# A two-layer attention and GLA trunk: small products of the first three head pairs at five stated places, rows of the position terms fetched between the first pass's loads

## The chip, the cores and the metric

The kernel runs on one core of one Trainium2 chip. The metric is the device time of one execution in microseconds (us); the kernel before takes 761.03 us, the median of 3 runs (760.69 to 761.86).

The engines are called by their names in the profile: PE is TensorE (matrix products, PEld its weight loads), DVE VectorE, ACT ScalarE, POOL GpSimd, SP SyncE, which here issues nearly all DMAs.

## The reference, cut to what matters

A trunk of two layers over 256 tokens with 1,024 features. Each layer is a token mixer and a gated FFN with a short convolution; both are modulated by terms computed from a vector c (a 1,024 x 12,288 product over both layers, of which each column is one dot product per output). Layer 0 mixes tokens by attention: 16 heads of width 64 in 3 groups, where group 0 sees every earlier token up to 128 back, and groups 1 and 2 see every 4th and every 16th. The change touches this attention.

```python
qkv = (h @ w_in).reshape(B, S, A_GROUPS, 3, A_HEADS, A_HEAD_DIM)
...
s = jnp.einsum('bnqrhe,bnkrhe->bnrhqk', qb, kk).astype(jnp.float32) + bias[None, None, None]
s = jnp.where(mask[None, :, None, None], s, NEG_INF)
m = jnp.max(s, axis=-1, keepdims=True)
p = jnp.exp(s - m)
den = jnp.sum(p, axis=-1)
o = jnp.einsum('bnrhqk,bnkrhe->bnqrhe', p, vv.astype(jnp.float32))
...
wts = jax.nn.softmax(jnp.stack(lses), axis=0)
o = jnp.sum(wts[..., None] * jnp.stack(outs), axis=0)
return o.reshape(B, S, A_WIDTH).astype(h.dtype) @ w_out
```

The bias is a table lookup by distance (the position terms). Layer 1 mixes by gated linear attention, which the change leaves alone. The FFN is `u = h @ w_up`, a 3-tap convolution along the tokens, `(silu(a) * b) @ w_down`.

## The kernel before

**Products.** Each large fp32 product is made of three products of parts: a factor is split into a high part (rounded, by a cast on ACT, `whi`, L176) and the rest (`wlo`, a subtraction on DVE, L182 or in two halves by `low_part`, L188), and `mm3` (L203 to L205) adds high by high, high by low and low by high. So every weight that is loaded costs one cast on ACT and one subtraction on DVE before the second and third product. Weights arrive through four buffers `raw` by SP's queue.

**Pairs.** The 16 heads are worked as 8 pairs u (the loop `for u in range(NPAIR)`, L665). For a pair the large products give q and k of each of the three groups g (PSUM tiles `pqk`, over 8 blocks kt of 128 features) and v (`pv`, two banks of 128 tokens). The small products follow: `scores` (L484) gives the four score tiles `s` (two heads by two halves of the tokens; shared and rest for group 0, L496 and L501, 64 x 64 pieces of groups 1 and 2, L511), adds the position terms and takes maxima on DVE (L531), exponentiates on ACT (L550) and normalises on DVE (`pn`, L542, L543); `turn` (L565) or `turn_all` (L579) transposes pn on PE into PSUM banks `t`, which ACT and DVE copy to `pt` (L567, L583); `outputs` multiplies pt by v (`po`, L592, L596) and splits the result (L603, L604).

**First pass** (L670 to L703). Pair 0 whole and q, k of pair 1 are computed together over kt, while the inputs h are made block by block. For each kt SP loads 1,024 KB of the modulation's weights (`ada_raw`, L135) and 960 KB of `w0` (L169). DVE makes two dot products with c (L142), the scaled block xr (L287), the low part of the first half of w0 (L188), the low part of h (L291), and the low part of the second half. ACT makes the two terms `mod` (L150 from the first dot, L152 from the second), the casts of the two halves, and hhi (L289).

**After it.** u=1 has only v left (48 products over 384 columns). u=2 has three groups of q and k (48 products over 256 columns each) and v; from u=3 on each pair has the same, with its small products in fixed places: `turn_all` of the pair before after group 1, and `scores` of the pair and `outputs` of the pair before, after v. For the first three pairs the small products stand at some ten places between those of other pairs. DVE also works off the remaining dot products, three after groups 0 and 2 (`next_half`).

**What sets the order.** A scheduler places the instructions on each engine, from their dependencies and the order of the program's text; `behind(...)` (L276) and `tc.issue_after` state that an instruction is not placed ahead of another on the queue. So the order in the text moves things that the text does not name.

**Position terms.** `rows` holds for each head one line of 768 terms; it goes to device memory (`rows_d`, L442) and is read back by `load_bias` (L370) so that each partition gets its own shift: for each half-head two DMAs of 64.5 KB (L379) and two of 32 KB (L380). Before, the store and the 16 DMAs of pairs 0 and 1 follow all loads of the first pass and the two of v's weights.

**FFN** (`ffn`). The first tile of w_up lies at columns 112 and 640 of a shared buffer; copies of h for kt 6 and 7 (`level`) are used in two of 22 blocks.

## Time and profile before

| | |
|---|---|
| median of 3 runs | 761.03 us (760.69 to 761.86) |
| the profiled execution | 761.25 us |
| its span, from the first to the last instruction | 759.5 us |
| PE busy | 750.5 us, 99% |
| DVE, ACT, POOL busy | 649.7, 484.9, 31.9 us |
| read from HBM | 185.06 MB, 245 GB/s over the span |
| granted TensorE clock | 0.999 |
| first pass | 13.6 to 56.7 us of the span |
| from there to the first product of u=3 | 56.7 to 104.2 us |

The times in the profile count from the start of the span. A timeline row gives start, length, engine, line, operation, what is written and read, and in brackets the idle time ahead of it and what ended that. A group's row gives the count, the busy time and the mean of one in ns, and the idle time ahead of the group with its releasers. Neighbouring rows of one engine overlap by some 0.1 us, since an instruction starts before the one ahead is fully out.

### The profile page before, as it was taken

The numbers are of one execution on the slowest core, as the hardware profiler recorded it, in microseconds if no ns is written. First come the engines' busy times: TensorE is split into PE (matmuls) and PEld (weight loads), VectorE is DVE, ScalarE is ACT, GpSimd is POOL, SyncE is SP. The second block draws the span as 40 slices with busy tenths as digits, with TensorE's granted clock in tenths as the row PEclk, the third lists the DMA queues.
The fourth block names the chain that finished last, engine by engine and source line by source line (L and its number), as shares of the span: only waits on it lengthen the run. The fifth ranks groups of instructions, "written<-read, shape, count | busy, mean of one in ns | idle before, by whom it ended". The sixth has DMA issues, their size and how long they took to land.

```text
span 759.5 us, 16068 instructions
## 1 busy us (share of the span) xinstructions
PE 750.5 (99%) x6416; PEld 732.3 (96%) x6416; DVE 649.7 (86%) x1190; ACT 484.9 (64%) x951; POOL 31.9 (4%) x57
## 2 busy tenths in 40 slices
PE   8999999999999999999999999999999999999997
PEld 6999899999999999999999999999999999999996
DVE  6997999888989679999999868987868999998592
ACT  6466666565556478676767556836867866676551
POOL 0001101101101010000000000000010000000100
PEclk9999999999999999999999999999999999999999
DMA  8988888878887357877646986864646777774621
GB/s 349 405 287 304 325 300 324 277 263 309 275 286 257 112 189 274 318 268 242 230 143 235 365 278 219 337 227 176 213 168 229 248 261 269 208 174 156 205 99 56
DMA packets 39481, 187.20 MB, mean 246 GB/s; under 512 B 9020, under 2 KB 11708, under 8 KB 25838
## 3 DMA queue, kind: packets, MB, share of 16 engines
q1 hardware_dynamic: 39024, 185.73, 70.4%
q8 instruction: 50, 0.82, 0.4%
q10 hardware_dynamic: 382, 0.45, 0.2%
q14 instruction: 25, 0.20, 0.1%
HBM read 185.06 MB, written 1.10 MB: 245 GB/s over the span
## 4 chain that ended last, share of the span: by engine, by line
PE 83%; DMA 7%; DVE 6%; ACT 2%; issue 1%; SPq 0%; ACTq 0%; DVEq 0%
PE pab L204 10%; PE pab L205 10%; PE pab L203 10%; PE pqk L203 5%; PE pqk L205 5%; PE pqk L204 4%; PE pd L204 4%; PE pd L205 4%; PE pd L203 4%; PE pv L203 3%; PE pv L205 3%; PE pv L204 3%; DMA raw<-in_w 2%; PE py L203 2%; PE py L205 2%; PE py L204 2%
## 5 line engine op out<-in xcount | busy, mean ns | idle before, releaser
L176 ACT CAST whi<-raw 128x1024 fp32r<-128x1024 f32 (+4 forms) x262 | 236.9, 948 | 100.8 <-PE pab L204 44.6
L182 DVE TENSOR_TENSOR wlo<-raw,whi 128x1024 fp32r<-128x1024 f32 (+5 forms) x246 | 263.2, 1096 | 37.3 <-ACT whi L176 36.5
L204 PE MATMUL pab<-hlo,whi 128*128 128x256 f32 x672 | 185.0, 277 | 0.0
L205 PE MATMUL pab<-hhi,wlo 128*128 128x256 f32 x672 | 184.9, 277 | 0.0
L203 PE MATMUL pab<-hhi,whi 128*128 128x256 f32 x672 | 183.5, 277 | 0.0
L204 PEld LDWEIGHTS pab<-hlo,whi 128*128 128x128 f32 x672 | 126.2, 188 | 0.2
L205 PEld LDWEIGHTS pab<-hhi,wlo 128*128 128x128 f32 x672 | 126.2, 188 | 0.0
L203 PEld LDWEIGHTS pab<-hhi,whi 128*128 128x128 f32 x672 | 125.2, 188 | 0.1
L142 DVE CUSTOM_DVE_ANT_0 ada_raw<-ada_raw,c_bc 128x1024 f32<-128x1024 f32 x96 | 114.3, 1233 | 3.2 <-DMA ada_raw<-in_w_ada 3.0
L203 PE MATMUL pqk<-hhi,whi 128*128 128x256 f32 x374 | 102.4, 279 | 0.0
L204 PE MATMUL pqk<-hlo,whi 128*128 128x256 f32 x374 | 102.0, 278 | 0.0
L205 PE MATMUL pqk<-hhi,wlo 128*128 128x256 f32 x374 | 101.6, 279 | 0.2 <-DVE wlo L182 0.2
L205 PE MATMUL pd<-ghi,wlo 128*128 128x256 f32 x308 | 84.8, 276 | 0.0
L204 PE MATMUL pd<-glo,whi 128*128 128x256 f32 x308 | 84.8, 276 | 0.0
L203 PE MATMUL pd<-ghi,whi 128*128 128x256 f32 x308 | 84.7, 276 | 0.0
L205 PEld LDWEIGHTS pqk<-hhi,wlo 128*128 128x128 f32 x374 | 69.2, 188 | 1.1 <-issue 0.7
L203 PEld LDWEIGHTS pqk<-hhi,whi 128*128 128x128 f32 x374 | 69.9, 188 | 0.2 <-ACT v L642 0.2
L204 PEld LDWEIGHTS pqk<-hlo,whi 128*128 128x128 f32 x374 | 69.9, 188 | 0.1
L205 PEld LDWEIGHTS pd<-ghi,wlo 128*128 128x128 f32 x308 | 57.7, 188 | 0.0
L204 PEld LDWEIGHTS pd<-glo,whi 128*128 128x128 f32 x308 | 57.7, 188 | 0.0
L203 PEld LDWEIGHTS pd<-ghi,whi 128*128 128x128 f32 x308 | 57.7, 188 | 0.0
L203 PE MATMUL pv<-whi,hhi 128*128 128x384 f32 (+2 forms) x160 | 53.1, 337 | 0.6 <-DVE k L616 0.3
(275 smaller groups left out, 1473.6 us busy)
## 6 DMA issues: line engine op xcount, KB each, us to landing
raw<-in_w_up SPq DMA_DIRECT2D x42, 1024.0 KB, 5.0
ada_raw<-in_w_ada SPq DMA_DIRECT2D x29, 1024.0 KB, 5.9
raw<-in_w_down SPq DMA_DIRECT2D x28, 704.0 KB, 4.4
ada_raw<-in_w_ada SPq DMA_DIRECT2D x38, 512.0 KB, 6.7
raw<-in_wqk SPq DMA_DIRECT2D x18, 1024.0 KB, 6.6
raw<-in_wv SPq DMA_DIRECT2D x14, 768.0 KB, 6.7
raw<-in_w SPq DMA_DIRECT2D x7, 960.0 KB, 6.5
raw<-in_w_v_b SPq DMA_DIRECT2D x6, 768.0 KB, 5.4
```

What stands on the lines that cost most here:

```text
L142: i = nc.vector.tensor_tensor_reduce(w, w, c_bc, op0=ALU.mult, op1=ALU.add, scale=1.0, scalar=0.0, accum_out=dot,)
L176: copied[0] = nc.scalar.copy(part(hi[:, c]), part(raw[:, c]))
L182: last_lo[0] = nc.vector.tensor_tensor(part(lo[:, c]), part(raw[:, c]), part(hi[:, c].bitcast(F32)), op=ALU.subtract)
L203: mm(ps, a[0], b[0], start=start, stop=False)
L204: mm(ps, a[0], b[1], start=False, stop=False)
L205: return mm(ps, a[1], b[0], start=False, stop=stop)
```

## The change

The store of the rows is issued after w0 of kt 2, and the four DMAs of one half-head after w0 of kt 3, 4, 5 and 6 each: pair 0's two half-heads, then pair 1's. In the loop, the small products of the first three pairs are stated at five places: scores of pair 0 after v of u=1; scores of pair 1 after group 0 of u=2; the transposes of pair 0 after group 1; those of pair 1 after group 2; and after v of u=2 the scores of pair 2 and the outputs of pairs 0 and 1. The normalisation of row 3 is no longer held back for the first two pairs. In the FFN the first tile of w_up lies at column 0, the copies of h are made for kt 6 alone, and in the two blocks that use them kt 6 is taken third.

```diff
@@ -365,13 +365,18 @@
     shift(att, 32)
     rows = att.tile([16, NROW], F32, tag="pt", name="rows")
 
-    def load_bias(u):
+    biases = [[], []]
+
+    first = []
+
+    def load_bias(u, heads=range(2)):
 
         both = []
         r = rows_d[:, :]
-        first = None if u else att.tile([P, 4, KEYS], F32, tag="pt", name="bias")
-        for hh in range(2):
-            b = (first[:, 2 * hh : 2 * hh + 2, :].rearrange("p a b -> p (a b)")[:, 0 : KEYS + 2] if u == 0
+        if u == 0 and 0 in heads:
+            first.append(att.tile([P, 4, KEYS], F32, tag="pt", name="bias"))
+        for hh in heads:
+            b = (first[0][:, 2 * hh : 2 * hh + 2, :].rearrange("p a b -> p (a b)")[:, 0 : KEYS + 2] if u == 0
                  else att.tile([P, KEYS + 2], F32, tag=f"bias{hh}", name="bias", bufs=1)[:, :])
             at = r.offset + (2 * u + hh) * NROW
             for x in range(2):
@@ -438,8 +443,13 @@
         if kt == 1:
             with behind(last):
                 last = scale_terms(1)
+        with tc.issue_after(last_load[0].ins):
+            if kt == 2:
+                nc.sync.dma_start(rows_d, rows)
+            elif 3 <= kt < 7:
+                u, hh = divmod(kt - 3, 2)
+                biases[u] += load_bias(u, (hh,))
     with tc.issue_after(last_load[0].ins):
-        nc.sync.dma_start(rows_d, rows)
         nc.sync.dma_start(small[:, C_CW:], I["small"][:, C_CW:])
 
     KO = 6
@@ -481,7 +491,7 @@
     last_pv, last_s, last_cast = [], [None], [None]
     OLEVEL = 5
 
-    def scores(u, q, k, v, bias):
+    def scores(u, q, k, v, bias, *after):
 
 
         m = tmp.tile([P, 16], F32, tag="m", name="m")
@@ -500,38 +510,36 @@
             e = slice(E * hh, E * hh + E)
             return mm(s[:, 0:n], qs[e, hh, P * (i // 2) : P * (i // 2) + P], kl[e, 0:n], start=False, stop=True)
 
-        def dilated(s, tiles):
+        def dilated(s):
...
 
 
 
-        for tiles in ((0, 1, 2), (3,)) if u == 0 else (range(4),):
-            s = {i: bank("s", "t" if i == 3 and u else "s") for i in tiles}
...
+        s = {i: bank("s", "t" if i == 3 else "s") for i in range(4)}
+        for i in range(4):
+            with behind(*after):
+                last = shared(s[i], i)
...
         pn = []
 
         def normalised():
@@ -550,7 +558,7 @@
                 exps.append(nc.scalar.activation(c, c, AF.Exp, bias=m[:, 4 + r : 5 + r], accum_out=m[:, 8 + r : 9 + r]))
             nc.vector.reciprocal(m[:, 12:16][:, rs], m[:, 8:12][:, rs])
             for r in (2 * hh, 2 * hh + 1):
-                if r < 3:
+                if u == 0 or u > 1 and r < 3:
                     normalised()
         return v, pn, normalised
 
@@ -565,7 +573,7 @@
                     last_t[0] = nc.tensor.transpose(t[:, c], pn[r][:, c], ident)
             with behind(*(evacuated if after else [])):
                 turned.append((nc.vector.tensor_copy if r % 2 else nc.scalar.copy)(pt[:, r, :], t[:, 0:KEYS]))
-            if r == 0:
+            if r == 0 and len(pn) < 4:
                 normalised()
 
     def turn_all(of, pt, *after):
@@ -577,7 +585,7 @@
             for i, (r, j) in enumerate(blocks[4 * n : 4 * n + 4]):
                 with behind(*after):
                     last_t[0] = nc.tensor.transpose(t[:, P * i : P * i + P], pn[r][:, P * j : P * j + P], ident)
-                if (r, j) == (0, 2):
+                if (r, j) == (0, 2) and len(pn) < 4:
                     normalised()
             with behind(*evacuated):
                 turned.append((nc.vector.tensor_copy if n == 1 else nc.scalar.copy)(flat[:, 512 * n : 512 * n + 512], t))
@@ -664,8 +672,7 @@
 
     for u in range(NPAIR):
         if u < 2:
-            with tc.issue_after(last_load[0].ins):
-                bias = load_bias(u)
+            bias = biases[u]
         place = u % 2 if u < 4 else 1
         if u == 0:
             k_hi, k_lo = ([att.tile([P, T + 4 * (i or j)], F32R, tag=f"k0{i}{j}", name="k", bufs=1) for j in range(2)] for i in range(2))
@@ -707,20 +714,22 @@
                     s, e = kt == 0, kt == KT - 1
 
 
-                    if u == 2 and (g, kt) == (1, 6):
-                        turn(before, pt := new_pt(), 0)
-                    at_t = u > 2 and (g, kt) == (2, 0)
                     hk = level if (u, g) > (3, 1) and g != 1 and kt == 0 else h[kt]
-                    with behind(*(last_t if at_t else [])):
+                    with behind(*(last_t if (g, kt) == (2, 0) else last_s if u == 2 and kt == 0 else [])):
                         mm3(pq[:, :T], parts(w, 2 * P * kt), hk, s, False)
                     mm_k = [mm3(pk[:, :T], parts(w, 2 * P * kt + P), hk, False, e)]
-                if g == 1 and u == 2:
-                    turn(before, pt, 1)
-                elif g == 1:
+                if g == 1:
                     turn_all(before, pt := new_pt(), *mm_k)
                 if (u, g) == (NPAIR - 1, 2):
                     copy_level((o_hi[OLEVEL], o_lo[OLEVEL]), *turned[-2:-1])
                 done = evacuate(q, k, g, pq, pk)
+                if (u, g) == (2, 0):
+                    second_pair = scores(1, *held, *mm_k)
+                elif (u, g) == (2, 1):
+                    for _ in range(4):
+                        second_pair[2]()
+                elif (u, g) == (2, 2):
+                    turn_all(second_pair, second_pt := new_pt(), *mm_k)
                 if (u, g) == (2, 0):
                     first_loads.append(last_load[0])
                 for _ in range((3, 0, 3)[g]):
@@ -736,7 +745,7 @@
                 with behind(*chain[7]):
 
 
-                    if half == 1 and u in (1, 3):
+                    if half == 1 and u < 4:
                         hi, lo = ((first_values,), ()) if u == 1 else (second[:1], second[1:])
                     else:
                         hi = lo = ()
@@ -749,22 +758,24 @@
                     wv = parts(w, 384 * k4, 384)
                     for t in range(2):
                         ht = [y[:, P * t : P * t + P] for y in h[kt]]
-                        last_pv[:] = [mm3(pv[t][:, :384], ht, wv, kt == 0, kt == KT - 1)]
+                        with behind(*(last_t if u == 2 and kt == 0 else [])):
+                            last_pv[:] = [mm3(pv[t][:, :384], ht, wv, kt == 0, kt == KT - 1)]
         for n in range(2):
             copies = by_group(v[n], pv[n], n)
             if u == n == 0:
                 first_values = copies
-        now = scores(u, q, k, v, bias)
         if u == 0:
-            pt = new_pt()
-            for half in range(2):
-                turn(now, pt, half)
-            outputs(0, now, pt)
-        elif u > 1:
-
-            outputs(u - 1, before, pt, last_s[0])
-            if u == 2:
-                copy_level(h[0], last_cast[0])
+            first_pair = q, k, v, bias
+            continue
+        if u == 1:
+            held = q, k, v, bias
+            before = scores(0, *first_pair, *last_pv)
+            continue
+        now = scores(u, q, k, v, bias, *last_pv)
+        outputs(0 if u == 2 else u - 1, before, pt, last_s[0])
+        if u == 2:
+            outputs(1, second_pair, second_pt, last_po[0])
+            copy_level(h[0], last_cast[0])
         before = now
     pt = new_pt()
     for half in range(2):
@@ -930,13 +941,10 @@
         if l == 0:
             raw = wraw.tile([P, 2048], F32, tag="raw", name="raw")
             nc.sync.dma_start(raw[:, 0 : KT * P], I["w_up"][l, 0][:, KT * P :])
-            own = shared
+            split_into([(raw[:, c : c + 512], shared[0][:, c : c + 512], shared[1][:, c : c + 512]) for c in (0, 512)])
+            w_early = [shared]
         else:
-            raw = wraw.tile([P, 2048], F32, tag="raw", name="raw")
-            last_load[0] = nc.sync.dma_start(raw[:, 0 : KT * P], I["w_up"][l, 0][:, KT * P :])
-            own = [wspl.tile([P, 2048], F32R, tag=tag, name=tag) for tag in ("whi", "wlo")]
-        split_into([(raw[:, c : c + 512], *(y[:, at : at + 512] for y in own)) for c, at in ((0, 112), (512, 640))])
-        w_early = [own]
+            w_early = [split(I["w_up"][l, 0][:, KT * P :], KT * P)]
         with behind(*sixth):
             w_early.append(split(I["w_up"][l, 1], 2048, low=() if l else last_x[1:], late=last_x[1:]))
         h, whole = all_normed(l, 1, "s", early)
@@ -946,7 +954,7 @@
             g_lo = [pool.tile([P, T], F32R, tag=f"glo{i}", name="glo", bufs=1) for i in range(NFF)]
 
             shift(pool, 8)
-            level = {kt: [pool.tile([P, T], F32R, tag=f"lv{kt}{s}", name="lv", bufs=1) for s in range(2)] for kt in (6, 7)}
+            level = {kt: [pool.tile([P, T], F32R, tag=f"lv{kt}{s}", name="lv", bufs=1) for s in range(2)] for kt in (6,)}
             for i in range(NFF):
                 if i == 2:
                     with behind(*chain[7]):
@@ -957,7 +965,7 @@
 
                     pab, pab1 = bank("pab", "t"), bank("pab")
                     for kt in range(KT):
-                        mm3(pab[:, :T], parts(w_early[0], P * kt + (112 if kt < 4 else 128)), h[kt], kt == 0, kt == KT - 1)
+                        mm3(pab[:, :T], parts(w_early[0], P * kt), h[kt], kt == 0, kt == KT - 1)
                         for s in range(2):
                             mm3(pab1[:, T * s : T * s + T], parts(w_early[1], 2 * P * kt + P * s), h[kt],
                                 kt == 0 and s == 0, kt == KT - 1 and s == 1)
@@ -971,7 +979,7 @@
                     pab = bank("pab")
                     pu = [pab[:, :T], pab[:, T:]]
 
-                    kts = range(KT)
+                    kts = (0, 1, 6, 2, 3, 4, 5, 7) if i in (2, 12) else range(KT)
                     for kt in kts:
                         hk = level.get(kt, h[kt]) if i in (2, 12) else h[kt]
                         for s in range(2):
```

What the scheduler makes of it, at the two places of which the prediction speaks.

**ACT in the first pass, kt 5 to 7.** The names are those above (`dot` the result of a dot product, `one_b`, `small` tables). One kt before:

```order
L150 ACTIVATE mod<-dot,one_b,small 128x1
L176 CAST whi<-raw 128x960
L152 ACTIVATE mod<-dot,small 128x1
L289 ACTIVATE hhi<-xr,mod 128x256
L176 CAST whi<-raw 128x960
```

and with the change:

```order
L150 ACTIVATE mod<-dot,one_b,small 128x1
L152 ACTIVATE mod<-dot,small 128x1
L176 CAST whi<-raw 128x960
L289 ACTIVATE hhi<-xr,mod 128x256
L176 CAST whi<-raw 128x960
```

The second mod has moved ahead of the first cast in these three kt; in the earlier ones, and on DVE in all, the order is as it was.

**PE and ACT in u=2.** On PE, the scores of pair 1 before, inside group 1 of u=2 and mixed with the outputs of pair 0:

```order
L592 MATMUL po<-pt,v 64x256
L496 MATMUL s<-q 128x258
L501 MATMUL s<-k,q 128x256 x2
L501 MATMUL s<-k,q 128x258 x2
L511 MATMUL s<-k,q 64x64 x4
L592 MATMUL po<-pt,v 64x256 x3
L596 MATMUL po<-pt,v 64x64 x8
L511 MATMUL s<-k,q 64x64 x12
```

and with the change, between group 0 and group 1:

```order
L205 MATMUL pqk<-hhi,wlo 128x256
L506 MATMUL s<-q 128x256 x2
L506 MATMUL s<-q 128x258 x2
L511 MATMUL s<-k,q 128x256 x2
L511 MATMUL s<-k,q 128x258 x2
L520 MATMUL s<-k,q 64x64 x16
L203 MATMUL pqk<-hhi,whi 128x256
```

The scores stand in one piece (so do those of pairs 0 and 2); the outputs of pairs 0 and 1 follow v of u=2, and the transposes stand as two blocks of twelve. On ACT, the rows around the first copies of the transposed tiles in u=2, before (the copies of 128x384 are those of pair 1; pair 0's stand further up):

```order
L152 ACTIVATE mod<-dot,small 128x1
L176 CAST whi<-raw 128x768 x2
L616 ACTIVATE q<-pqk 128x256
L550 ACTIVATE prob,m<-prob,m 128x384 x2
L550 ACTIVATE prob,m<-prob,m 128x386 x2
L176 CAST whi<-raw 128x1024 x2
L616 ACTIVATE q<-pqk 128x256
L567 COPY pt<-t 128x384 x2
```

and with the change (pair 0's, 128x512 each):

```order
L176 CAST whi<-raw 128x768 x2
L152 ACTIVATE mod<-dot,small 128x1 x2
L176 CAST whi<-raw 128x768
L624 ACTIVATE q<-pqk 128x256
L176 CAST whi<-raw 128x768
L591 COPY pt<-t 128x512
L152 ACTIVATE mod<-dot,small 128x1
L558 ACTIVATE prob,m<-prob,m 128x384 x2
L591 COPY pt<-t 128x512
```

The first copy of a transposed bank now stands behind two mod, of which the second needs the second of the three dots that DVE makes after group 0, and behind the casts of the second half of v's weights.

36 lines of the change are left out of this document (16 added, 20 removed).

## The prediction

> **What bounds the kernel now.** I read the page first, then the table of windows by stage, then the timelines of the engines inside the two stages that the change touches. On the page and in the windows the columns are busy time (and, in a window, after its length: PE, PEld, DVE, ACT, POOL, granted clock, DMA share, GB/s).
>
> ```profile
> PE 750.5 (99%) x6416; PEld 732.3 (96%) x6416; DVE 649.7 (86%) x1190; ACT 484.9 (64%) x951; POOL 31.9 (4%) x57
> ```
>
> ```profile
> 13.60:56.70 43.10, 42.97 (x339) 42.48 (x338) 42.21 (x66) 25.64 (x50) 1.68 (x4) 1.00 0.94 357
> 56.70:104.20 47.50, 46.70 (x434) 43.14 (x432) 42.45 (x92) 31.93 (x70) 4.91 (x9) 1.00 0.89 327
> ...
> 20.00:48.00 28.00, 27.87 (x220) 27.46 (x219) 27.31 (x43) 14.44 (x25) 0.00 (x0) 1.00 1.00 392
> 48.00:53.00 5.00, 5.00 (x41) 4.92 (x40) 4.94 (x9) 3.63 (x7) 0.00 (x0) 1.00 0.96 303
> ```
>
> TensorE is busy 99% of the span, so time is won only where it does less or goes back to back more tightly, and lost wherever it must wait. But the share is an average. In the first pass (13.6 to 56.7) VectorE is busy 42.21 of 43.10 us as well, and the DMA is full (share 1.00 at 392 GB/s): three resources stand level. In the second stage (56.7 to 104.2, from the last product of the first pass to the first of u=3) VectorE is busy 42.45 of 47.50 us. So this stage can be shortened by about 5 us before VectorE alone would forbid it, and only if nothing waits for VectorE at a bad place.
>
> Who sets the pace in the first pass is seen in kt 5. ScalarE, then VectorE, then TensorE:
>
> ```profile
> 38.17 0.39 ACT L150 ACTIVATE mod<-dot,one_b,small 128x1 f32<-128x1 f32 x1 [2.37 <-DVE dot L142]
> 38.46 0.99 ACT L176 CAST whi<-raw 128x960 fp32r<-128x960 f32 x1
> 39.35 0.28 ACT L152 ACTIVATE mod<-dot,small 128x1 f32<-128x1 f32 x1
> 39.77 0.51 ACT L289 ACTIVATE hhi<-xr,mod 128x256 fp32r<-128x256 f32 x1
> 40.19 0.98 ACT L176 CAST whi<-raw 128x960 fp32r<-128x960 f32 x1
> ```
>
> ```profile
> 38.05 1.22 DVE L142 CUSTOM_DVE_ANT_0 ada_raw<-ada_raw,c_bc 128x1024 f32<-128x1024 f32 x1
> ...
> 39.20 0.48 DVE L287 SCALAR_TENSOR_TENSOR xr<-x_all,mod,rstd 128x256 f32<-128x256 f32 x1
> 39.59 1.15 DVE L188 TENSOR_TENSOR wlo<-raw,whi 128x960 fp32r<-128x960 f32 x1
> ...
> 42.28 1.22 DVE L142 CUSTOM_DVE_ANT_0 ada_raw<-ada_raw,c_bc 128x1024 f32<-128x1024 f32 x1
> ...
> 46.90 1.16 DVE L188 TENSOR_TENSOR wlo<-raw,whi 128x960 fp32r<-128x960 f32 x1 [0.38 <-ACT whi L176]
> ```
>
> ```profile
> 40.34 0.98 PE L691 MATMUL pqk<-hhi,whi 128*128 128x256 f32 x6
> ```
>
> ScalarE finishes hhi at 40.28, and TensorE starts kt 5's products at 40.34, 0.06 us later: the chain dot, mod, xr, hhi sets the start of each kt, and VectorE has no gap between its rows that could take up a delay.
>
> **The change, part by part.** *First pass, ScalarE's order.* With the loads of the position terms among those of the first pass, ScalarE's queue in kt 5, 6 and 7 is mod, mod, whi, hhi, whi, where before it was mod, whi, mod, hhi, whi. The second mod needs the second dot, whose row starts at 38.05 and which leaves VectorE at 39.27. The first cast therefore starts behind that mod, at 39.35 + 0.28 less the 0.09 by which neighbours overlap (38.46 + 0.99 = 39.45 against the next start 39.35), so at 39.54 instead of 38.46, and ends at 40.53. Two things hang on it. hhi starts at 40.44 instead of 39.77, which is 0.67 us later. wlo (39.59 now) can start at about 40.6, 1.0 us later; the low part of h and the second wlo stand behind it in VectorE's queue, so the first dot of the next kt (42.28) is 1.0 us late too. For kt 5 that is +1.0. For kt 6 it is +1.0 less about 0.33, because wlo already waited 0.38 us there (row at 46.90). For kt 7 only hhi counts, +0.67, since the rest of the kt is TensorE's. Sum **+2.35 us**; its bounds are 0 (were the casts off the path) and 2.7 (without the deduction).
>
> *First pass, the rows.* Each half-head fetches 2 x 64.5 KB and 2 x 32 KB, 0.198 MB. At 392 GB/s that is 0.50 us; in the window 48 to 53, where seven such DMAs were issued among loads, 303 GB/s moved instead of 392, a shortfall of 5 x 89 = 445 KB, so 1.14 us over seven or 0.65 per half-head. So one costs the DMA between 0.50 and 1.15 us, four cost 2.0 to 4.6. The loads of one kt (1024 + 960 KB, 2.03 MB) take 5.18 us at 392 GB/s and the engines take 43.10 / 8 = 5.39 a kt, so the loads gain some 0.2 a kt, 0.8 in four, and ScalarE's new order gives them another 2.35 us. From 2.0 to 3.15 is hidden under these; at 4.6 some 1.45 us sticks out. I take the low end, because the rows move in a stage where nothing but bytes was seen to count (share 1.00): **+0**, bounds 0 and +1.45. If the new order of ScalarE cost nothing, up to 4.6 - 0.8 = 3.8 would show.
>
> ```profile
> bias<-rows_d SPq DMA_DIRECT2D x8, 64.5 KB, 3.1
> ```
>
> ```profile
> bias<-rows_d SPq DMA_DIRECT2D x2, 64.5 KB, 5.8
> ```
>
> These two rows are the median time to landing of such a DMA, over all of 42 to 62 us and for the two issued first, behind the loads of w_v. The Trainium skill, "DMA: Bandwidth & Descriptors", section "Queues, rings and completion order", says that SyncE's DMAs share one ring on each DMA engine and that descriptors are consumed in ring order. That speaks against the change: rows put ahead of a load delay it by all they take. The trace agrees (5.8 us behind loads against 3.1). By the rule the sum stays as above; were rows and loads served side by side, the upper bound of 1.45 would fall away.
>
> *Second stage, the products.* The steps of TensorE are read from rows; one 384-column product takes a third of 58.95 - 58.43, one of 256 columns a third of 87.13 - 86.79; a block of scores lasts from 101.10 to 102.74, of outputs from there to 104.22, twelve transposes from 115.22 to 116.45.
>
> ```profile
> 58.43 0.34 PE L203 MATMUL pv<-whi,hhi 128*128 128x384 f32 x1
> 58.95 0.34 PE L203 MATMUL pv<-whi,hhi 128*128 128x384 f32 x1
> ...
> 86.79 0.28 PE L203 MATMUL pqk<-hhi,whi 128*128 128x256 f32 x1
> 87.13 0.28 PE L203 MATMUL pqk<-hhi,whi 128*128 128x256 f32 x1
> ...
> 101.10 0.65 PE L496 MATMUL s<-q 128*128 128x256 f32 x4
> ...
> 102.74 1.08 PE L592 MATMUL po<-pt,v 128*64 128x256 f32 x8
> ...
> 104.22 0.39 PE L203 MATMUL pqk<-hhi,whi 128*128 128x256 f32 x1
> ...
> 115.22 1.47 PE L579 MATMUL t<-ident,pn 128*128 128x128 f32 x12
> 116.45 0.36 PE L203 MATMUL pqk<-q,whi 128*128 128x256 f32 x1
> ```
>
> As five blocks, with no wait: 96 x 0.1734 = 16.65 (both passes of v), 144 x 0.1134 = 16.33 (q and k of u=2), 3 x 1.64 + 2 x 1.48 + 2 x 1.23 = 10.34, some 0.6 for the wait for the copies of v at the start, which stays, and six returns to long products at 0.11 (0.39 against 0.28 in the row at 104.22): 0.66. Sum 44.6 against 47.5: **-2.9 us**.
>
> *Second stage, the waits that take its place.* Count from S, the end of the first block of scores. q and k of group 0 (48 products, 5.45), a return, scores (1.64), a return and group 1 put the twelve transposes of pair 0 at S + 12.8. They fill PSUM banks of four transposes each. The third four, due at S + 13.6, go into the bank of the first four, so they are held until ScalarE has copied that one (the copy of 128x512). In ScalarE's queue this copy stands behind the second mod, which needs VectorE's second dot.
>
> ```profile
> L182 DVE TENSOR_TENSOR wlo<-raw,whi 128x1024 fp32r<-128x1024 f32 x11 | 13.1, 1218 | 3.2 <-ACT whi L176 3.2
> L142 DVE CUSTOM_DVE_ANT_0 ada_raw<-ada_raw,c_bc 128x1024 f32<-128x1024 f32 x6 | 7.2, 1248 | 0.0
> ...
> L542 DVE TENSOR_SCALAR pn<-prob,m 128x256 f32<-128x256 f32 x8 | 3.6, 456 | 0.1
> ...
> L543 DVE TENSOR_SCALAR pn<-prob,m 128x128 f32<-128x128 f32 x8 | 2.3, 287 | 0.0
> L531 DVE CUSTOM_DVE_ANT_0 prob<-s,bias 128x386 f32<-128x386 f32 x4 | 2.1, 552 | 0.1
> ...
> L625 DVE SCALAR_TENSOR_TENSOR q<-pqk,q 64x256 fp32r<-64x256 f32 x4 | 1.7, 422 | 0.1
> ```
>
> VectorE's queue from S to there, each mean less 0.08 of overlap: 6 sums of scores and rows at 0.47 = 2.8; 4 wlo at 1.14 = 4.6; 4 pairs of pn at 0.38 + 0.20 = 2.3; the evacuation of q and k, 3 at 0.34 = 1.0; four small ones 0.3; 2 dots at 1.17 = 2.3. Sum 13.3, none of it with a wait, as every input is there earlier (the loads come early now, and the exps need 1.5 us a pair). Then ScalarE:
>
> ```profile
> L176 ACT CAST whi<-raw 128x768 fp32r<-128x768 f32 x5 | 4.0, 834 | 1.9 <-issue 1.9
> ```
>
> ```profile
> L583 ACT COPY pt<-t 128x512 f32<-128x512 f32 x10 | 5.8, 578 | 0.0
> ```
>
> mod 0.28, whi 0.83, q about 0.4, whi 0.83, copy 0.58, less 0.09 four times, and 0.1 for two hand-overs: 2.7. So the bank is free at S + 16.0, and TensorE stands **2.4 us**. Bounds: 0 (if VectorE runs 2.4 us ahead of this sum) and 3. Later, the last transposes of pair 1 need the pn of rows 2 and 3, which VectorE reaches at about the time that TensorE does: **+0.2**, bounds 0 and 1. The second bank of v waits for the copy of k behind two wlo; it comes due some 1.5 us after that copy, so +0.
>
> In the Trainium skill, "TensorE: Matmul & The Clock Gate", Part 1, an idle window of about 3.4 us halves the clock; the granted clock is 1.00 in every window above, and no run here shows a stall that long. By that page 2.4 us would stay under it.
>
> *The two FFN.* The edits take away one pair of copies of h per layer and reorder products. None adds a product. I take 0, with bounds of 0.5 us either way.
>
> **Sum**, against the profiled execution (761.25 us, of which 759.5 are the span; the median of the runs is 761.03): +2.35 + 0 - 2.9 + 2.4 + 0.2 = +2.05, so **763.3 us**, in its own bounds 762.0 to 764.3.
>
> **The rivals.** *A, not slower: the third bank is not held.* Place: the transposes of pair 0. If VectorE reaches the second dot by S + 10.9 instead of S + 13.3, TensorE does not wait, and -2.9 + 2.35 - 0.1 gives 760.6. For it: VectorE's busy means may overlap more than 0.08. Against it: the sum has 26 rows with no gap. *B: ScalarE's order costs nothing*, because the loads of w0 land so late that the cast waits for them whichever way; then the bytes of the rows decide, 0 to 1 us, minus 0.3: 761.0 to 762. Against it: DMA and VectorE are level now, and the cast at 38.46 waited only for mod. *Both A and B*: 758.3. *C, dearer*: the rows cost 1.15 us a half-head (+1.45), or the FFN 0.5, or the last transposes 1.0: 764.5 to 766.
>
> **How the numbers follow.** A measurement of this kernel tells about 0.2% (1.5 us) from no change. Chances: the forecast 0.48, A 0.12, B 0.10, both 0.13, C 0.17. Faster by over 0.2% is "both", 0.13; within 0.2% A and B, 0.22; slower 0.65. The range leaves out "both" and the end of C: 760.3 to 766.0.
>
> **What would show it.** Right: hhi of kt 5 to 7 starts behind a whole whi cast, the first pass ends 2 to 3 us later; a wait of 2 to 3 us stands at the transposes after group 1, released by ScalarE's copy of pt; the stage from there to u=3 is about as long as before; the rest of the timeline is merely shifted. Wrong: a first pass of unchanged length, no wait at those transposes, waits of TensorE on loads, or an FFN whose length changes by over 0.5 us.

## The result, and the profile after

The changed kernel takes 769.99 us (median of 6 runs, 766.91 to 771.74) against 760.85 for the kernel before (6 runs, 760.47 to 761.86): 1.0115 times as long, with an interval of 1.009 to 1.0141. The forecast was 763.3 with a range to 766.0. The direction was right; the size, and the range, were not.

The profiled execution took 768.67 us, its span 766.9 against 759.5. First the page's busy times, then the windows of the changed kernel, cut at the same events as those of the kernel before: end of the first pass, first product of u=3, first product of the FFN of layer 0, first product of that of layer 1, end. The second fence has the kernel before in the three windows that the prediction did not show.

```profile
PE 752.5 (98%) x6416; PEld 735.1 (96%) x6416; DVE 649.2 (85%) x1188; ACT 483.6 (63%) x947; POOL 31.5 (4%) x57
```

```profile
13.60:60.60 47.00, 43.69 (x338) 42.62 (x338) 41.90 (x65) 25.25 (x48) 1.06 (x3) 1.00 1.02 374
60.60:109.70 49.10, 45.91 (x437) 43.87 (x435) 43.23 (x95) 32.06 (x71) 3.80 (x10) 0.97 0.80 292
109.70:289.70 180.00, 180.00 (x1596) 174.95 (x1591) 149.26 (x299) 107.38 (x244) 17.52 (x22) 1.00 0.70 241
289.70:581.40 291.70, 291.70 (x2441) 287.51 (x2439) 254.52 (x446) 196.40 (x375) 5.93 (x11) 1.00 0.69 246
581.40:766.90 185.50, 179.91 (x1582) 179.31 (x1580) 152.58 (x275) 114.27 (x202) 2.36 (x2) 0.99 0.61 193
```

```profile
104.20:281.20 177.00, 177.00 (x1595) 172.03 (x1591) 150.83 (x303) 106.63 (x241) 16.09 (x22) 1.00 0.73 251
281.20:573.40 292.20, 292.20 (x2441) 288.01 (x2439) 254.42 (x446) 197.81 (x377) 6.04 (x11) 1.00 0.70 246
573.40:759.50 186.10, 180.41 (x1582) 179.82 (x1580) 152.09 (x274) 114.72 (x204) 2.36 (x2) 1.00 0.61 192
```

The first column after the window is its length. So the first pass grew by 3.9 us (43.1 to 47.0), the stage of u=2 by 1.6 (47.5 to 49.1), the rest of layer 0's attention by 3.0 (177.0 to 180.0), and the two windows that begin with an FFN shrank by 0.5 and 0.6. The sum is 7.4. The third term is the odd one: TensorE is busy in all of it in both kernels, no instruction was changed there, and it takes 3.0 us more.

TensorE's waits between 13 and 110 us (us in total, times, longest):

```profile
PE pqk L698 <- ACT hhi L289: 3.3, 5, 0.8
PE t L587 <- ACT pt L591: 2.4, 1, 2.4
PE pv L203 <- ACT v L650: 0.8, 1, 0.8
```

**The wait that was forecast.** Here is the chain of VectorE's second dot, ScalarE's row and TensorE's transposes, from three timelines of the changed kernel:

```profile
84.30 1.23 DVE L142 CUSTOM_DVE_ANT_0 ada_raw<-ada_raw,c_bc 128x1024 f32<-128x1024 f32 x1
```

```profile
85.58 0.29 ACT L152 ACTIVATE mod<-dot,small 128x1 f32<-128x1 f32 x1 [0.85 <-DVE dot L142]
85.78 0.82 ACT L176 CAST whi<-raw 128x768 fp32r<-128x768 f32 x1
86.50 0.37 ACT L624 ACTIVATE q<-pqk 128x256 f32<-128x256 f32 x1
86.78 0.82 ACT L176 CAST whi<-raw 128x768 fp32r<-128x768 f32 x1
87.50 0.58 ACT L591 COPY pt<-t 128x512 f32<-128x512 f32 x1
```

```profile
88.14 0.66 PE L587 MATMUL t<-ident,pn 128*128 128x128 f32 x4 [2.43 <-ACT pt L591]
...
89.24 0.41 PE L205 MATMUL pqk<-hhi,wlo 128*128 128x256 f32 x1
89.46 0.41 PE L203 MATMUL pqk<-hhi,whi 128*128 128x256 f32 x1
```

```profile
88.90:92.40 3.50, 3.50 (x20) 3.50 (x19) 3.46 (x11) 1.58 (x6) 0.00 (x0) 0.54 0.88 323
92.60:95.60 3.00, 3.00 (x29) 3.00 (x27) 2.28 (x9) 1.01 (x4) 0.00 (x0) 1.00 1.01 292
```

The third group of transposes waits 2.43 us, by the steps that were written down. What was not is behind it: from 89.2 products follow at 0.21 us instead of 0.115; the granted clock is 0.50 for 3.4 us (0.54 over the 3.5 us shown), and at 92.6 it is 1.00 again. Seventeen products lose 0.1 us each, 1.6 to 1.7 us.

**The pace.** Every third product of group 1 of u=4, before and after, the first and the last of fifteen rows:

```profile
139.37 0.28 PE L203 MATMUL pqk<-hhi,whi 128*128 128x256 f32 x1
...
144.13 0.28 PE L203 MATMUL pqk<-hhi,whi 128*128 128x256 f32 x1
```

```profile
145.65 0.28 PE L203 MATMUL pqk<-hhi,whi 128*128 128x256 f32 x1
...
150.60 0.28 PE L203 MATMUL pqk<-hhi,whi 128*128 128x256 f32 x1
```

42 products take 4.76 us before (113.3 ns each) and 4.95 after (117.9). A row's own length is 0.28 in both; only the distance of the starts shows it. From the scores of one pair to those of the next it takes 29.79 us instead of 29.25, 2.7 us over u=3 to 7; the rest of the third term, 0.2 to 0.3, lies behind the scores of the last pair.

**The first pass.** ScalarE in kt 3 and in kt 5 of the changed kernel:

```profile
28.77 1.00 ACT L176 CAST whi<-raw 128x960 fp32r<-128x960 f32 x1 [1.03 <-DMA raw<-in_w]
...
41.21 0.29 ACT L152 ACTIVATE mod<-dot,small 128x1 f32<-128x1 f32 x1 [0.76 <-DVE dot L142]
41.41 0.98 ACT L176 CAST whi<-raw 128x960 fp32r<-128x960 f32 x1
42.29 0.51 ACT L289 ACTIVATE hhi<-xr,mod 128x256 fp32r<-128x256 f32 x1
```

The loss begins in kt 3, where ScalarE's order is that of before: the cast waits 1.03 us for its load. From hhi to hhi, kt 3 to 7 take 6.4, 6.3, 6.0, 6.5 and 6.2 us, against 5.5, 5.4, 5.4, 5.7 and 5.4 before. The fetches also keep SyncE's queue: the load of the modulation's weights that follows kt 3's w0 is issued at 25.13 us instead of 23.03. But the DMA engines did not run out of work for it: with the rows in flight their share stays at 0.98 while the rate falls (26 to 28 us, before and after):

```profile
26.00:28.00 2.00, 2.00 (x17) 2.00 (x17) 2.00 (x4) 0.58 (x2) 0.00 (x0) 1.00 1.06 432
```

```profile
26.00:28.00 2.00, 2.00 (x18) 2.00 (x17) 2.00 (x4) 0.39 (x1) 0.00 (x0) 1.00 0.98 263
```

### The profile page after: what moved, and what is told of

It reads as the page before. It is cut to its first block, busy times and chain, and to the rows that moved or that the text cites. A ratio compares the mean times of both kernels' runs of the same rounds, so it can differ in the third digit from the quotient of the medians.

```text
span 766.9 us, 16065 instructions
## 1 busy us (share of the span) xinstructions
PE 752.5 (98%) x6416; PEld 735.1 (96%) x6416; DVE 649.2 (85%) x1188; ACT 483.6 (63%) x947; POOL 31.5 (4%) x57
## 4 chain that ended last, share of the span: by engine, by line
PE 88%; DMA 6%; DVE 4%; ACT 2%; issue 0%; SPq 0%; DVEq 0%; ACTq 0%
PE pab L204 10%; PE pab L203 10%; PE pab L205 10%; PE pqk L203 6%; PE pqk L205 5%; PE pqk L204 5%; PE pd L203 4%; PE pd L205 4%; PE pd L204 4%; DMA raw<-in_w 4%; PE pv L203 4%; PE pv L205 4%; PE pv L204 4%; PE py L203 2%; PE py L205 2%; PE py L204 2%
## 5 line engine op out<-in xcount | busy, mean ns | idle before, releaser
L205 PE MATMUL pab<-hhi,wlo 128*128 128x256 f32 x680 | 187.0, 276 | 0.0
L204 PE MATMUL pab<-hlo,whi 128*128 128x256 f32 x680 | 186.9, 276 | 0.0
L205 PE MATMUL pqk<-hhi,wlo 128*128 128x256 f32 x374 | 103.2, 283 | 0.0
L993 ACT ACTIVATE r<-pab,small 128x256 f32<-128x256 f32 x86 | 47.4, 561 | 9.7 <-DVE r L996 9.3
```

Of the source, the lines that this page charges most:

```text
L204: mm(ps, a[0], b[1], start=False, stop=False)
L205: return mm(ps, a[1], b[0], start=False, stop=stop)
L993: nc.scalar.activation(r, u[:, :T], AF.Identity, scale=cw[2], bias=col(C_CB + 44 * l + f))
```

## The experiments

The theory formed from this comparison: (1) the rows' fetches cost the first pass 4 us because the loads are its bound; (2) the regrouped products gain what was counted and lose it to one wait and a withheld clock; (3) u=3 to 7 are slower because the position terms' tiles moved q, k, v, prob and pn to other addresses; (4) the FFN's edits gain 1 us. The rivals stand in the expectations. All medians below are of runs beside runs of the kernel before on the same chip, whose medians lay between 760.4 and 761.1.

**after_again**: the changed kernel, unedited.

> The changed kernel once more, on the chip of the three runs beside it. Its six runs lay between 766.9 and 771.7 us, its profiled run at 768.7. Theory (addresses): in that run 4.1 us were lost in the first pass, 2.4 in a wait at the transposes of pair 0, 1.7 in 17 products at half clock behind that wait, and 2.7 because the 256-column products of u=3 to 7 take 117.8 ns instead of 113.4, while the FFN gained 1.0; a run near 771 should show the same terms and one more of about 3 us of the same kind (a stage at the slower pace, or another stretch at half clock). Rival (order): the same time for the same reason in each run, spread by noise of the loads in the first pass; then the first pass alone differs between runs.

Measured: 767.58 us (4 runs, 766.72 to 768.44), profiled at 768.11 with nearly the same terms: last hhi at 54.8, the wait 2.43, u=3 to 7 at 117.8 ns. The clock's term is smaller: its 3.4 us at 0.50 begin at 87.7, inside the wait, so that ten products run slowly and not seventeen, 0.9 us instead of 1.6.

```profile
87.70:91.10 3.40, 3.13 (x15) 3.13 (x16) 3.40 (x10) 2.19 (x7) 0.00 (x0) 0.50 0.74 249
```

Of the ten runs of this kernel seven lie between 766.7 and 768.7 and three between 771.3 and 771.8. No run of the upper group was profiled. The experiments show two things that add some 3 us to single runs: a slow stretch of the second FFN (ffn_alone) and a full clock that comes late at the start (addresses_alone). Which of them those three runs had is not shown.

**addresses_alone**: the kernel before, with pair 1's tiles created ahead.

```diff
+    second_bias = [att.tile([P, KEYS + 2], F32, tag=f"bias{hh}", name="bias", bufs=1) for hh in range(2)]
+
     def load_bias(u):
...
+                 else second_bias[hh][:, :] if u == 1
                  else att.tile([P, KEYS + 2], F32, tag=f"bias{hh}", name="bias", bufs=1)[:, :])
```

> The kernel before with the two tiles of pair 1's position terms created at the start, so that they lie ahead of q, k, v, prob and pn in the on-chip memory, as in the changed kernel; no instruction changes its place on any engine. Addresses theory: u=3 to 7 at 117.8 ns for the 256-column products, 0.54 us a pair: about 763.5 us, the first 104 us unchanged. Order theory: no difference, 761.0 us.

Measured: 763.21 us (5 runs, 762.47 to 765.64), 1.004 (1.0024 to 1.0056). With the same instructions in the same order, addresses 3136 bytes up cost 2.8 us. From pair to pair it takes 29.8 us in u=4 to 7, as in the changed kernel, against 29.25; in u=3 only group 2 is slower (29.4). The profiled run is the longest of the five, 765.64, because TensorE's full clock came late in it, at 18.8 us instead of some 10: the twelve small products ahead of the first pass take 2.93 us, twice the usual, and the first pass starts 3.0 us later. Before, and in this run:

```profile
12.22 1.60 PE L301 MATMUL warm<-ones_d 128*128 128x128 f32 x12
13.58 0.95 PE L691 MATMUL pqk<-hhi,whi 128*128 128x256 f32 x6
```

```profile
14.00 2.93 PE L301 MATMUL warm<-ones_d 128*128 128x128 f32 x12
16.58 1.63 PE L694 MATMUL pqk<-hhi,whi 128*128 128x256 f32 x6
```

The order on the engines is the same in both, and the other four runs are 1.4 to 3.2 us shorter, so this is put down to the run and not to the edit.

**up_64_bytes**: the kernel before, one padding longer by 64 bytes a partition.

```diff
-    shift(att, 56)
+    shift(att, 64)
```

> The kernel before with all tiles behind one padding moved up by 64 bytes a partition (q, k, v, prob, pn, and the three spare weight tiles), and nothing else. 3136 bytes are 24 and a half times 128. Theory (parity of 64): the slower pace in u=3 to 7 comes with this as well, about 763.3 us. Rival: the pace depends on more than the remainder by 128, then 760.9, or a slow pace in other stages only.

Measured: 763.48 us (10 runs, 763.08 to 764.36), 1.003 (1.0021 to 1.0039); from group 2 of u=3 on the products follow at 117.8 ns. So 64 bytes do what 3136 do. The granted clock of this run is 1.00, so this is not the clock.

**rows_elsewhere**: the changed kernel, with pair 1's terms in the second buffer of the transposed tiles, so that q, k, v, prob and pn lie where they did before.

```diff
-        if u == 0 and 0 in heads:
+        if u < 2 and 0 in heads:
...
-            b = (first[0][:, 2 * hh : 2 * hh + 2, :].rearrange("p a b -> p (a b)")[:, 0 : KEYS + 2] if u == 0
+            b = (first[u][:, 2 * hh : 2 * hh + 2, :].rearrange("p a b -> p (a b)")[:, 0 : KEYS + 2] if u < 2
```

> The changed kernel with pair 1's position terms in the second buffer of the transposed tiles instead of tiles of their own, so that q, k, v, prob and pn have their addresses of before; the order on every engine is that of the changed kernel. Addresses theory: u=3 to 7 at 113.4 ns, 2.7 us less than the changed kernel: about 764.5 us (first pass and stage as there). Rival: the changed kernel's slower pace has to do with its new blocks too, then 767.5.

Measured: 764.23 us (7 runs, 763.35 to 767.97), 1.0047 (1.003 to 1.0064). The pairs are back at 29.25 us (113.4 ns) with the new order in place, u=3 included. The third term is the addresses' alone, shown from both sides. (The profiled run, 767.97, has the slow stretch of the second FFN, below. Its wait at the transposes is 2.03 us, and 3.4 us at a clock of 0.50 follow that as well.)

**all_but_q** and **q_only**: the kernel before with 64 bytes of padding behind the q tiles of group 0 (`shift` of 8 columns), and with such a padding on both sides of them. These tiles also hold the copies of h (`level`, `copy_level`) that the first kt of groups 0 and 2 reads from group 2 of u=3 on.

```diff
+    shift(att, 8)
     level = []
     q_pair = []
...
+    shift(att, 8)
+
     def copy_level(y, *after):
```

The first of the two lines stands in q_only alone.

> The kernel before with 64 bytes of padding behind the q tiles of group 0 (which also hold the copies of h that some products read) and so ahead of k, v, prob, pn and the rest; the order is that of before on every engine. If the q tiles of group 0 set the pace, nothing changes: 761.0 us. If the tiles of the small products behind them do (k, v, prob, pn), u=3 to 7 run at 117.8 ns: about 763.5.

> The kernel before with the q tiles of group 0 moved by 64 bytes and all behind them by 128. If the q tiles of group 0 set the pace: about 763.5 us. If the tiles behind them do, by the remainder by 128: 761.0 us. If both kernels are slow, what counts is how the two lie to each other; if neither, the spare weight tiles ahead of them, which up_64_bytes moved as well.

Measured: all_but_q 761.76 us (10 runs, 760.67 to 764.67), 1.0018 (1.0006 to 1.003), the pairs at 29.25 us; its profiled run, 764.66, has the late clock of addresses_alone (first pass from 17.4 us), and takes 0.6 us more behind the last pair's scores. q_only 763.71 us (4 runs, 763.38 to 764.02), 1.0041 (1.0026 to 1.0056): u=3 takes 29.2 us, u=4 to 7 take 29.8 each, at 117.8 ns. So the place of the tiles that hold group 0's q and the copies of h decides from u=4 on. (The tiles behind them moved by 128 bytes in q_only and by 64 in all_but_q; 128 bytes alone were not tried.) Whether q or the copies count was not separated.

**rows_alone**: the kernel before with only the store and the 16 fetches moved.

```diff
...
+        with tc.issue_after(last_load[0].ins):
+            if kt == 2:
+                nc.sync.dma_start(rows_d, rows)
+            elif 3 <= kt < 7:
+                u, hh = divmod(kt - 3, 2)
+                biases[u] += load_bias(u, (hh,))
     with tc.issue_after(last_load[0].ins):
-        nc.sync.dma_start(rows_d, rows)
```

> The kernel before with only the store and the 16 fetches moved among the first pass's loads. Theory: the last hhi comes 4 us later, of it 0.9 each in kt 3 and kt 4, where the cast waits for its load, and the rest in kt 5 to 7; the tiles of q, k and v lie 3136 bytes further up and u=3 to 7 run at 117.8 ns, +2.7: about 767.5 us. Order theory: only the 4 us: about 765. If the rows cost nothing and the cast's place alone does, kt 3 and 4 are unchanged and the sum is about 763.

Measured: 767.4 us (4 runs, 767.13 to 767.7), 1.009 (1.0074 to 1.0107). Last hhi at 54.8 (50.8 before), and 117.8 ns from group 2 of u=3 on. This part alone costs as much as the whole change in its quicker runs; what the rest gains and loses there comes out even.

**cast_first**: the changed kernel, with the first cast of w0 emitted ahead of the second mod, so that ScalarE's order in kt 5 to 7 is that of before.

```diff
+        if kt:
+            raw = wraw.tile([P, 2048], F32, tag="raw", name="raw")
+            last_load[0] = nc.sync.dma_start(raw[:, 0 : 15 * P], I["w0"][kt])
...
+            with behind(dots[0][1]):
+                cast.append(nc.scalar.copy(parts0[0][:, 0:960], raw[:, 0:960]))
         with behind(dots[0][0]):
-            dots.append(ada_dot(0, kt, 1, ada))
+            dots.append(ada_dot(0, kt, 1, ada, cast))
...
```

> The changed kernel with the first cast of w0 put back ahead of the second mod in every kt, the rows' fetches left where they are. Loads theory: a kt now moves 2.03 MB and 0.2 MB of rows at about 350 GB/s, 6.3 us, which is what kt 3 to 6 take, so the cast then waits for its load instead: last hhi at 54.2 to 54.9 us (54.8 in the changed kernel), total within 0.7 us of the changed kernel's 767.6. Rival (order theory of the prediction): the casts' place costs 0.7 us a kt, so the last hhi comes at 52.5 to 53 us and the total is 2 us less.

Measured: last hhi at 54.64, total 770.29 us (4 runs, 768.91 to 772.52). The first pass is what it was; the casts now wait for their loads (kt 5, 6 and 7):

```profile
41.41 1.00 ACT L433 CAST whi<-raw 128x960 fp32r<-128x960 f32 x1 [0.82 <-DMA raw<-in_w]
47.78 0.99 ACT L433 CAST whi<-raw 128x960 fp32r<-128x960 f32 x1 [0.99 <-DMA raw<-in_w]
53.41 1.00 ACT L433 CAST whi<-raw 128x960 fp32r<-128x960 f32 x1 [0.26 <-DMA raw<-in_w]
```

The cast of kt 5 starts at 41.41 in both kernels, once because of mod and once because of the load. So the loads hold the first pass, and the changed order hid behind them; only in kt 7, behind the last rows, does the old order gain (5.6 us against 6.2), and the last hhi comes 0.1 to 0.3 earlier than in the two profiles of the changed kernel. The total is not within 0.7 us, since the order of the stage behind moved too (in the profiled run a wait of 2.9 at the transposes, with 3.4 us at a clock of 0.50 behind it, one of 0.5, and the FFN's slow stretch, below).

**dots_later**: the changed kernel, with u=2's first three dots made after group 1.

```diff
-                for _ in range((3, 0, 3)[g]):
+                for _ in range(((0, 3, 3) if u == 2 else (3, 0, 3))[g]):
```

> The changed kernel with the three dot products of u=2's group 0 made after group 1 instead, so that the copy of the first transposed bank no longer stands behind them. Theory: the wait of 2.4 us at the transposes of pair 0 shrinks to under 0.7, and with it goes the stretch at half clock (17 products, 1.7 us): about 763.5 us. Rival 1: the wait goes and the half clock stays, as it has another reason: 765.2. Rival 2: the dot products hold something else as long a little later (the last transposes of pair 1, or the copy of k): 766 to 768.

Measured: 771.05 us (4 runs, 768.98 to 772.11). The second rival. At the transposes of pair 0 the wait is down to 0.4, but those of pair 1 wait for pn, and the clock falls behind that instead:

```profile
PE t L587 <- DVE pn L550: 2.7, 1, 2.7
...
PE t L587 <- DVE m L539: 0.4, 1, 0.4
```

```profile
95.60:99.00 3.40, 3.40 (x14) 3.27 (x13) 3.40 (x7) 0.88 (x2) 0.00 (x0) 0.50 1.00 358
```

VectorE has so much to do in this stage that what is taken from one place stands at the next. From the last hhi to the outputs it takes 53.0 us against 52.0; the rest of the distance to the changed kernel is the FFN's slow stretch (below), which the profiled run has.

**filled_wait**: the changed kernel, with 24 transposes more in the wait; they write again what the second four wrote (`fill` is set for u=2 alone).

```diff
-                    last_t[0] = nc.tensor.transpose(t[:, P * i : P * i + P], pn[r][:, P * j : P * j + P], ident)
+                    for _ in range(7 if n == 1 and fill else 1):
+                        last_t[0] = nc.tensor.transpose(t[:, P * i : P * i + P], pn[r][:, P * j : P * j + P], ident)
```

> The changed kernel with 24 transposes more (the second four, seven times over into the same bank, 2.6 us of work), at the place where TensorE waits 2.4 us. Theory: TensorE is busy through the wait, no clock is withheld, and the 17 products behind it run at 113 to 118 ns instead of 213: the stage is 1.7 us shorter although work was added. Rival: the granted clock falls for another reason (the mean load, or the end of the transposes), then it falls here too, and the time is that of the changed kernel or longer.

Measured: the window behind the wait, as above:

```profile
87.50:91.00 3.50, 3.50 (x34) 3.45 (x32) 3.50 (x9) 2.29 (x7) 0.00 (x0) 1.00 0.77 245
```

Clock 1.00, and 34 products and transposes in 3.5 us where the changed kernel had 20 products. From the last hhi to the outputs it takes 50.4 us instead of 52.0, though work was added. The idle time is what withheld the clock. The runs' median is 767.50 (766.70 to 770.12) against 767.58: the 1.6 us of the profile are not separated from the scatter by the runs.

**rows_back**: the changed kernel, with the store and the fetches behind the first pass's loads again.

```diff
-            elif 3 <= kt < 7:
-                u, hh = divmod(kt - 3, 2)
-                biases[u] += load_bias(u, (hh,))
     with tc.issue_after(last_load[0].ins):
+        nc.sync.dma_start(rows_d, rows)
...
-            bias = biases[u]
+            with tc.issue_after(last_load[0].ins):
+                bias = load_bias(u)
```

> The changed kernel with the store of the rows and the 16 fetches put back behind the first pass's loads. Addresses theory: the tiles of the position terms are again placed behind q, k and v, so the products of u=3 to 7 are back at 113.4 ns; the first pass is as before (last hhi at 50.8 us); the stage up to u=3 keeps its wait and half clock (about +1.5 against before) and the FFN its gain of 1.0: about 761 us. Order theory: the slower pace comes from the new order of small products, so 117.8 ns stays in u=3 to 7: about 764 us.

Measured: 765.39 us (4 runs, 762.66 to 765.93), 4.4 us above the addresses theory and 1.4 above the order theory. First pass and pace are as expected (last hhi 0.4 later than before, the pairs at 29.25), but the stage of u=2 takes 3.4 us more than before. The second FFN of the profiled run has the slow stretch, below, 2.5 us. The weights of u=2 again come behind the rows, and the regrouped products find them missing:

```profile
PE pqk L205 <- DVE wlo L182: 2.5, 2, 1.8
PE pqk L203 <- ACT v L645: 1.0, 1, 1.0
PE pv L203 <- ACT v L645: 0.9, 2, 0.5
PE t L582 <- DVE pn L545: 0.6, 1, 0.6
```

So the two parts belong together: without early rows the regrouping costs 3.4 us there, with them 1.5; and early rows cost 4 in the first pass. The wait of 1.8 us here was not followed by a lower clock (1.00 from 87 to 92 us).

**ffn_alone**: the kernel before with all three edits of the FFN.

```diff
...
-            level = {kt: [...] for kt in (6, 7)}
+            level = {kt: [...] for kt in (6,)}
...
-                        mm3(pab[:, :T], parts(w_early[0], P * kt + (112 if kt < 4 else 128)), h[kt], kt == 0, kt == KT - 1)
+                        mm3(pab[:, :T], parts(w_early[0], P * kt), h[kt], kt == 0, kt == KT - 1)
...
-                    kts = range(KT)
+                    kts = (0, 1, 6, 2, 3, 4, 5, 7) if i in (2, 12) else range(KT)
```

> The kernel before with the three edits of the FFN alone. Theory: the 256-column products at the start of each FFN run at 113.4 ns instead of 117.8, some 0.5 us per layer, so 1.0 us in all: about 759.7 us against 760.6. Rival: the gain of 1.0 seen in the changed kernel came from what stands ahead of the FFN, then no difference.

Measured: ten runs in two groups, four from 759.69 to 760.18, five from 762.13 to 762.80, and one at 764.66. The profiled run (762.13) is of the upper group. The window from 580 to 640 us in the kernel before and in this run:

```profile
580.00:640.00 60.00, 60.00 (x529) 60.00 (x528) 56.96 (x98) 43.89 (x76) 0.00 (x0) 1.00 0.76 260
```

```profile
580.00:640.00 60.00, 60.00 (x512) 60.00 (x511) 56.31 (x96) 42.12 (x72) 0.00 (x0) 1.00 0.75 259
```

TensorE is busy throughout at clock 1.00 in both, and does 17 products fewer in the second (some records can be missing, but the starts agree: 117.8 ns apart instead of 113.3 from 576 to 640). The slow stretch ends at the thirteenth block, where the copies of h are used again. From its first to its last product with w_up the second FFN takes 117.8 us before, 117.3 in the changed kernel and 119.8 here; it takes 119.8 in the profiled runs of rows_elsewhere, rows_back, cast_first and dots_later too. So the 1 us is there, and with it a chance of 2.5 us lost.

**early_tile_alone**: the first of these edits alone.

```diff
...
-                        mm3(pab[:, :T], parts(w_early[0], P * kt + (112 if kt < 4 else 128)), h[kt], kt == 0, kt == KT - 1)
+                        mm3(pab[:, :T], parts(w_early[0], P * kt), h[kt], kt == 0, kt == KT - 1)
```

> The kernel before with one edit of the FFN: its first tile of w_up lies at column 0 of its buffers instead of 112 and 640. No instruction changes its place, and no other tile its address. Theory: the start of each FFN runs at the faster pace, 0.5 us a layer, and no run has the slow stretch of 576 to 640 us: about 759.7 us in every run. Rival: the gain or the slow stretch comes with this edit; then the runs split into 759.8 and 762.5, as with all three edits.

Measured: 760.13 us (12 runs, 759.56 to 762.86), 0.9985 of the kernel before (0.9972 to 0.9998), eleven of the twelve between 759.56 and 761.25. Each FFN takes 117.4 us instead of 117.8. This is the best version found: 0.15% below the kernel before, an interval that barely leaves out no difference.

**level_alone**: the other two edits.

> The kernel before with the other two edits of the FFN: copies of h for kt 6 alone, and kt 6 taken third where they are used. Theory: these make the slow stretch of the second FFN (113.4 to 117.8 ns from the third block to the thirteenth, 2.5 us) a matter of chance, so the runs split into about 760.8 and 763.3. Rival: the stretch needs the moved tile; then all runs lie near 760.8.

Measured: 760.52 us, 0.9999 (0.9982 to 1.0015); six of the runs between 760.18 and 760.55, three at 763.5 to 763.6 (a tenth took 1861 us and is left out). So the moved tile is not needed for such a step: of the runs with the copies and the order of kt changed (ffn_alone, level_alone) nine of 19 lie in an upper group, with the moved tile alone one of 12. The kernel before is not free of it: of its 32 runs on this chip five lie between 763.3 and 764.1. None of these was profiled, so for them the slow stretch is not told from the late clock of addresses_alone.

## Why the prediction was wrong

- *ScalarE's order, +2.35, and the rows, +0: together 3.9 to 4.1 measured, above the bound of 3.8 that the prediction itself gave for the rows where the order is free.* Two steps failed. The first: four half-heads were set against slack that "gains 0.2 a kt" and against the order's 2.35 us. But the order changes only from kt 5 on, and the first two half-heads come in kt 3 and 4, where nothing covered them: 0.9 us in each. The second: 0.50 us a half-head was taken from the bytes, at 392 GB/s. A window of the changed kernel over the kt with rows shows the rate itself lower at full DMA share (32 to 50 us, before and after):

```profile
32.00:50.00 18.00, 17.87 (x140) 17.56 (x139) 17.50 (x27) 9.36 (x17) 0.00 (x0) 1.00 0.99 369
```

```profile
32.00:50.00 18.00, 15.87 (x121) 15.24 (x121) 15.10 (x24) 8.66 (x15) 0.00 (x0) 1.00 1.04 341
```

A kt of 2.03 + 0.2 MB at 341 GB/s takes 6.5 us; 6.0 to 6.5 were measured. ScalarE's order came as forecast (in kt 5 to 7 each kt is 0.6 to 0.8 us longer) but did not set the time: cast_first takes it back and gains at most 0.3 us.
- *The products of the second stage, -2.9: right.* From start to start and without waits, the small products cost 10.3 us as blocks (10.34 forecast) against 11.8, the large ones, returns included, 1.0 less (the half clock set apart), and waits of 0.24 and 0.30 are gone: -3.0.
- *The held third bank, +2.4: right, 2.43, by the chain that was named.* The last transposes of pair 1, +0.2: no wait was seen. The wait for the copies of v was to stay as it was; it went from 0.26 to 0.76.
- *The withheld clock: named and put aside, with 0.* The prediction took the Trainium skill, "TensorE: Matmul & The Clock Gate", Part 1, to mean that an idle time under some 3.4 us is free. The trace says otherwise: after 2.43 us of waiting the clock was 0.50 for 3.4 us, 1.7 us lost. That the loss lasts as long as the window of the Trainium skill's page agrees with it; that a whole window must be idle does not. filled_wait shows that the idle time was the cause.
- *u=3 to 7: nothing forecast, +3.0 measured.* The prediction took it that "the rest of the timeline is merely shifted", so that work not named in the change keeps its pace. The diff creates the tiles of pair 1's terms earlier, and that moves q, k, v, prob and pn by 3136 bytes. addresses_alone and up_64_bytes give +2.8 and +2.4 with no other difference, and rows_elsewhere takes it away.
- *The FFN, 0 with bounds of 0.5: -1.1 in the profiled run.* Most of the gain of 0.5 a layer is the moved tile's (0.4 in early_tile_alone; 0.2 in level_alone). Against it stands a stretch of 2.5 us at the slower pace that comes in some runs only: ffn_alone's upper runs lie 1.1 to 1.8 us above the kernel before. The three runs of the changed kernel above 771 lie about as far from the others, though none of them was profiled.
- *The rivals.* B had the right mechanism for the casts, which wait for their loads whichever way they are ordered (cast_first: 0.82 and 0.99 us in kt 5 and 6), but priced the rows at 0 to 1 us. C, "dearer", had the price: 1.15 us a half-head makes 3.8 us of first pass, against 3.9 measured. Neither stood in the sum, which put the rows at 0. None of the rivals had a change of pace where no instruction changes, and that, with the clock, is most of what lies between C's 764.5 to 766 and 768.

The forecast's own sum was +2.05. The profiled run: +1.6 more in the first pass, +0.5 for v, +1.7 for the clock, +3.0 for the pace, -1.1 for the FFN, -0.2 for the last transposes make +7.5 (its span: +7.4).

What sets the pace is settled in part. From u=4 on, 64 bytes in the place of the tiles with group 0's q and the copies of h decide it (q_only, all_but_q), and a group keeps the pace it began with, though after its first kt it reads h itself. That the copies are what counts is not shown, and they are not the whole of it: in the changed kernel groups 0 and 1 of u=3 already run at 117.8 ns, and no product reads a copy before group 2. rows_elsewhere takes these two groups back to 113.3 as well; in up_64_bytes and addresses_alone they never left it. Why 64 bytes do this stays open, and so does why the second FFN falls into the slower pace in some runs and not in others.

## What to carry to other kernels

Work that is moved among loads must be covered at the place where it lands, not by slack that comes later; when DMA share is already 1.00, take the rate with small pieces from a window that has some. A wait of TensorE has a second price behind it, the withheld clock, so look at the granted clock in the 3.4 us after each wait of 2 us or more. And compare the addresses of tiles, not only the order of instructions: a tile that is created earlier moves all behind it, and a kernel that was timed with one placement has to be timed again with the other.

## What the runs showed of the hardware

- The 256-column products follow at 113.3 or at 117.8 ns, with granted clock 1.00 in both, and nothing between holds for long. Which one is taken depends, from u=4 on, on 64 bytes in the place of the tiles with group 0's q and the copies of h (q_only, all_but_q), and in the FFN of layer 1 on the run (ffn_alone). The 384-column products take 173 ns in either.
- Waits of TensorE of 2.43 us (the changed kernel, twice), 2.03 (rows_elsewhere), 2.86 (cast_first) and 2.67 (dots_later) each brought 3.41 us at a granted clock of 0.50, which began between 0.3 us before the wait's end and 1.0 us after it; one of 1.78 in rows_back brought none. Transposes in the gap kept it at 1.00.
- In these traces the clock changes only on a grid: in the changed kernel its first stretch at full clock lasts 78.51 us, 23 times 3.413, and in every run each stretch at full clock is a whole number of such steps. In the step ahead of each of the five half clocks TensorE was idle for 2.03 to 2.83 us of 3.41; the wait of rows_back fell across two steps, with 1.30 us in the fuller one. So what a wait costs depends on how it lies on the grid: 17 slow products in one run of the changed kernel, ten in the other. Where between 1.30 and 2.03 us the limit lies, no run shows.
- The full clock came at some 9 to 11 us of the span in 14 of the 16 profiled runs and at 18.8 and 19.6 in two (addresses_alone, all_but_q), which moved the first pass by 3.0 and 3.8 us.
- Fetches of 0.2 MB a kt in short rows brought the DMA from 369 to 341 GB/s at full share (32 to 50 us), and from 432 to 263 within the 2 us shown above. In kt 3 the load of w0, issued ahead of the first fetch, was late as well, which the order of issue alone does not explain; what held it was not tried.
